# Second attention products of several token tiles in one row: a two-block fp32 kernel on one core

## The chip, the cores and the metric

The kernel runs on one core of one Trainium2 chip. The core has a matrix engine (TensorE, PE in the profile; its weight loads stand apart as PEld), three engines for elementwise work (VectorE or DVE, ScalarE or ACT, GpSimd or POOL) and a queue that only issues transfers (SyncE, SP). Each engine takes its instructions in the order of the program, and they wait for each other by semaphores. The metric is the device time of one execution in microseconds (us).

## The reference

Two transformer blocks on 1024 tokens of width 1024, in float32. What matters here is the attention, which comes in three kinds, and one small product:

```
# block 1: 8 heads of 64, banded to 256 keys per 128 queries, with sinks
m = maximum(max(scores), sink); e = exp(scores - m)
out = einsum(e / (sum(e) + exp(sink - m)), v_band)
# block 2, kind a: 8 heads, up to 640 keys per 128 queries, relative bias
probs = softmax(q @ k.T / 8 + bias);   out = probs @ v
# block 2, kind b ("stick breaking"): 8 heads, all earlier keys
weights = where(strict, exp(log_sigmoid(l) + log_tail), 0);  out = weights @ v
# modulation of block 2: one row of 6144 numbers
mod = silu(c) @ w_ada + b_ada
...
ff = square(relu(h @ w_ff1)) @ w_ff2     # the modulation is computed during this
```

## The kernel before

Nothing in the source is issued at once. A recording layer (`Recorder`) takes every instruction down; `flush` then orders them with a list scheduler that holds an estimated cost for each engine, gives a free engine the ready instruction that was recorded first, and issues the result as a fixed program. All instructions therefore carry one line number in the profile (L390, the line that calls them), and tiles are told apart by name.

Large matrix products are split: each float32 operand is a high and a low part, and three products of the parts are added (operands `128x512`, called large products below). The second product of the attention isn't split: the probabilities of a tile of 128 queries are transposed on PE in blocks of 128x128 (`PS<-cst,F`, `cst,Q`, `cst,e`, with the identity as `cst`), copied from PSUM (`PS`) to a buffer `pT` by ACT or DVE, and multiplied with V (`PS<-pT,v`). Such a product with V writes 64 rows of `PS`: one head of a pair fills rows 0 to 63, the other 64 to 127. The profile records each of them twice, so `x16` in a row of its timeline is 8 products.

The work on a pair of heads is a unit: four in block 1 (`attn1`), then four of kind b (`attn_b`), then four of kind a (`attn_a`). In a unit the tiles t = 0 to 7 follow each other: scores, softmax or stick breaking, and `pv_pair`, which takes two key blocks at a time: four transposes, one copy, four products, and then the next two blocks. There are two `pT` buffers, and every third copy is DVE's. Four tiles share one bank of PSUM for their outputs, which `o_evac` (or the end of `attn1`) empties.

PE has other work meanwhile: the large products for q and k of the next unit (`PS<-ga,low`, `PS<-low`) and, in the last unit, the first half of the output product (`PS<-low,ga`), whose operand is loaded from `d_o` into the buffers `ga` as soon as the last q and k products have read them.

The stage of `w_ff1` (products in a Winograd scheme, some 84 large products for each pair of column blocks p) computes the modulation on the side. `ada_unit` loads 256 KB of `w_ada` into one of two halves of a buffer `fxt`, and DVE multiplies it into an accumulator; after eight of them two products with a column of ones (`PS<-fxt,ones`) sum the accumulator, once for each of 12 groups.

In `attn_a` a bias tile is made for each head from a small transfer (`pT<-d_ext`), and the exponentials lie in six buffers that `attn_b` uses too.

Of the kernel before, what the change touches and what calls it, by code (L numbers as in the profile page):

```python
# [9 lines left out]
F32 = mybir.dt.float32  # L10
# [77 lines left out]
class Recorder:  # L88
# [23 lines left out]

    SIZES = {"pT": 512, "aff": 256, "ss": 2}
# [134 lines left out]
    def link(self, idx):  # L248
# [156 lines left out]
def two_blocks_kernel(ctx: ExitStack, tc: tile.TileContext, a, out, dbg=None):  # L405
# [432 lines left out]
    def pv_pair(pool, o, ocol, v, vsl, pt, kbs, t0):  # L838


        first, last = kbs[0], kbs[-1]
        for i in range(0, len(kbs), 2):
# [4 lines left out]
            sb = rec.tile(pool, [P, 512], F32, "pT", 2, uniq("pT"))  # L847
# [5 lines left out]
            j = 0  # L853
            for kb in grp:
                for hf in (0, 1):
                    PE.matmul(o[64 * hf:64 * hf + 64, ocol], v[:, kb, vsl(hf)], sb[:, j * P:j * P + P],
                              start=(kb == first), stop=(kb == last))
                    j += 1

    def attn1(i, qs):  # L860
        c = i // 2
        for t in range(NT):
# [28 lines left out]
            if t % 4 == 0:  # L891
                o = ps_o()
            ocol = slice((t % 4) * P, (t % 4) * P + P)
            kbs = list(range(t - nb + 1, t + 1))
            pv_pair(p1, o, ocol, v1, lambda hf: slice(64 * c, 64 * c + 64),
                    lambda hf, kb: e[:, hf, (kb - kbs[0]) * P:(kb - kbs[0] + 1) * P], kbs, t)
            if t % 4 == 3:
                oh = rec.tile(p1, [P, 2, 512], F32R, "oh", 2, uniq("oh"))
                ACT.copy(oh[:, 0, :], o)
                DVE.tensor_tensor(oh[:, 1, :], o, f32(oh[:, 0, :]), ALU.subtract)  # L900
                c0 = (t // 4) * 512
                SP.dma_start(f32(d_o1[i][:, :, c0:c0 + 512]), f32(oh))
# [6 lines left out]


    for t in range(NT):
# [5 lines left out]
        st = p1f()  # L917
        for n, sl in enumerate(halves):
            g = ps_g()
            gemm_N_half(g, [(pt[:, 0, k], pt[:, 1, k]) for k in range(2)], [ws.slot(I_PLE + k) for k in range(2)], n)  # L920
            ACT.copy(st[:, sl], g)
        SP.dma_start(d_ple[t], st)
# [307 lines left out]
    ada_units = [(g_, k) for g_ in range(12) for k in range(8)]  # L1230

    def ada_unit(g_, k):
        acc, w = hs(fx[0])[g_ % 2], hs(fx[1])[k % 2]
# [5 lines left out]
        if k == 7:  # L1239
            o = View.of(R_8, uniq("ada"))  # L1240
            brow = rec.tile(ff, [P, 256], F32, "aff", 1, uniq("brow"))
            for j in range(2):
                pr = slice(32 * j, 32 * j + 1)
                PE.matmul(o[pr, 0:256], ones1, acc[:, 256 * j:256 * j + 256], start=True, stop=True)
            for j in range(2):
                pr, at = slice(32 * j, 32 * j + 1), 512 * (g_ % 2) + 256 * j
                SP.dma_start(brow[pr, :], a["b_ada_2"][0:1, (g_ // 2) * 1024 + at:(g_ // 2) * 1024 + at + 256])
                DVE.tensor_tensor(brow[pr, :], o[pr, 0:256], brow[pr, :], ALU.add)
                SP.dma_start(d_ada[g_ // 2:g_ // 2 + 1, at:at + 256], brow[pr, :])
# [14 lines left out]
    def ff1_evac(p, c1, c2):  # L1264
# [6 lines left out]
        for _ in range(8 if p > 2 else 0):  # L1271
            if ada_units:
                ada_unit(*ada_units.pop(0))
# [198 lines left out]
    R_F = Ring([p7.tile([P, 1024], F32, name=f"F{i}") for i in range(4)] + [res[i] for i in (4, 5)])  # L1472
    res67 = resx[3].rearrange("p a b -> p (a b)")
    R_bA = Ring([res67[:, 640 * i:640 * i + 640] for i in range(3)])
# [48 lines left out]
    def attn_b(i, qs, ks, kl, v):  # L1523
        for t in range(NT):
# [18 lines left out]
            if t % 4 == 0:  # L1543
                o = ps_o()
            pv_pair(p7, o, slice((t % 4) * P, (t % 4) * P + P), v, lambda hf: slice(64 * hf, 64 * hf + 64),
                    lambda hf, kb: wts[hf][:, kb * P:kb * P + P], list(range(t + 1)), t)
            if t % 4 == 3:
                o_evac(4 + i, t, o, cst[:, C_GB + i:C_GB + i + 1])

    def attn_a(i, qs, ks, kl, v):  # L1550
        bias = []
        for hf in (0, 1):
            h = 2 * i + hf
            hk = rec.tile(p7, [P, 256], F32, "pT", 2, uniq("hk"))
            src = d_ext[h]
            SP.dma_start(hk, bass.AP(tensor=src.tensor, offset=src.offset + 1, ap=[[1, P], [1, 256]]))
            b = View.of(R_bA, uniq("bA"))
            DVE.tensor_copy(b[:, 0:384], hk[:, 255:256].to_broadcast([P, 384]))
            DVE.tensor_copy(b[:, 384:640], hk[:, ::-1])
            DVE.memset(b[0:64, 576:640], NEG)  # L1560
            DVE.memset(b[64:128, 0:64], NEG)
            bias.append(b)
        for t in range(NT):
            nb = min(t, 4)
            k0, nk, b0 = (t - nb) * P, (nb + 1) * P, (4 - nb) * P
            es = [p7f(), p7f()]
# [18 lines left out]
            if t % 4 == 0:  # L1585
                o = ps_o()
# [214 lines left out]
```

## Time and profile before

| | |
|---|---|
| median of 3 runs | 2362.85 us (2362.24 to 2362.9) |
| the profiled execution's own time | 2360.25 us |
| its span in the profile | 2358.5 us |
| PE busy / PE weight loads / DVE / ACT / POOL | 96% / 77% / 76% / 47% / 28% |
| block 1 attention, about | 111 to 192 us |
| stage with the modulation, about | 420 to 657 us |
| kind b attention, about | 1198 to 1413 us |
| kind a attention, about | 1413 to 1600 us |

The span is what the trace covers; the time of the execution is 1.75 us longer, and the median of the runs 2.6 us above that execution. Rows of the timeline merge equal instructions that follow each other; the start of a row less the start of the row before it is what the earlier row took of PE, since the lengths that are shown overlap.

### The profile page before, as it was taken

What the parts mean: (1) busy time and instruction counts of PE and PEld (TensorE: products, weight loads), DVE (VectorE), ACT (ScalarE), POOL (GpSimd) and SP (SyncE); (2) the same over time, 40 slices, a digit from 0 to 9 for tenths busy, and PEclk for the clock granted to TensorE, in tenths of its full rate; (3) what the DMA queues carried; (4) which work ended last, traced back from release to release, by engine and by line L of the source; (5) the groups of instructions that cost most, each with busy time, mean ns of one, the idle gap of its engine ahead of it and who ended that gap; (6) DMA issues with size and microseconds to landing.
All of it is one profiled execution on the core that took longest, in us unless ns stands there. A gap on an engine that the chain in (4) does not pass through costs nothing.

```text
span 2358.5 us, 30684 instructions
## 1 busy us (share of the span) xinstructions
PE 2259.0 (96%) x11201; PEld 1819.6 (77%) x11201; DVE 1783.6 (76%) x2613; ACT 1105.7 (47%) x1966; POOL 654.5 (28%) x541
## 2 busy tenths in 40 slices
PE   7999999999999999999999999989899999999996
PEld 6777878777778888887877777767788888887885
DVE  6464497777677889946779986663888878779897
ACT  3264275445455340055546665530855555546412
POOL 5443200000034233624535443352100000003365
PEclk9999999999999999999999999999999999999998
DMA  5529146666562316232062233363322222234123
GB/s 199 150 87 350 54 139 223 229 200 211 193 234 72 143 31 207 73 119 81 12 210 76 73 93 97 86 208 103 119 92 93 83 81 87 83 126 173 41 98 134
DMA packets 109463, 304.53 MB, mean 129 GB/s; under 512 B 11296, under 2 KB 22784, under 8 KB 106368
## 3 DMA queue, kind: packets, MB, share of 16 engines
q1 hardware_dynamic: 109312, 302.57, 38.8%
q8 instruction: 88, 1.44, 0.3%
q14 instruction: 63, 0.52, 0.1%
HBM read 211.26 MB, written 74.49 MB: 121 GB/s over the span
## 4 chain that ended last, share of the span: by engine, by line
PE 74%; DVE 10%; DMA 8%; ACT 3%; issue 2%; POOL 2%; SPq 0%; POOLq 0%; DVEq 0%; ACTq 0%
PE PS L390 74%; DMA fxt<-in_w_ada_dram 4%; DVE Q L390 3%; DVE low L390 2%; ACT Q L390 1%; DVE fxt L390 1%; POOL low L390 1%; DMA gu<-lt 1%; DMA wr<-in_w_in_dram 1%; DMA gu<-d_r 1%; DVE F L390 0%; DMA sc<-in_xT_dram 0%; DMA ga<-d_o 0%; DMA pT<-d_ext 0%; ACT low L390 0%
## 5 line engine op out<-in xcount | busy, mean ns | idle before, releaser
L390 PE MATMUL PS<-low 128*128 128x512 f32 x2868 | 686.0, 392 | 5.3 <-ACT low L390 3.7
L390 PEld LDWEIGHTS PS<-low 128*128 128x128 f32 x2868 | 537.1, 189 | 117.5 <-ACT low L390 5.2
L390 PE MATMUL PS<-ga,low 128*128 128x512 f32 x1488 | 394.0, 403 | 18.4 <-ACT ga L390 6.6
L390 PEld LDWEIGHTS PS<-ga,low 128*128 128x128 f32 x1488 | 279.6, 193 | 78.3 <-issue 14.4
L390 POOL TENSOR_TENSOR ra<-ga 128x1024 f32<-128x1024 f32 x9 | 25.2, 2801 | 786.0 <-DMA ga<-in_w_down_dram 413.1
L390 PE MATMUL PS<-gu,low 128*128 128x512 f32 x744 | 178.2, 392 | 4.5 <-POOL gu L390 4.5
L390 PEld LDWEIGHTS PS<-gu,low 128*128 128x128 f32 x744 | 140.0, 189 | 36.1 <-POOL gu L390 5.0
L390 ACT CAST low<-Q 128x512 fp32r<-128x512 f32 (+1 forms) x148 | 94.3, 640 | 151.0 <-PE PS L390 106.1
L390 PE MATMUL PS<-low,gu 128*128 128x512 f32 (+2 forms) x640 | 149.0, 384 | 2.3 <-DMA gu<-lt 1.0
L390 DVE SCALAR_TENSOR_TENSOR fy<-Q,cst,fy 128x1023 f32<-128x1023 f32 (+1 forms) x88 | 116.8, 1329 | 39.6 <-ACT fy L390 38.8
L390 PEld LDWEIGHTS PS<-low,gu 128*128 128x128 f32 x640 | 115.9, 188 | 26.5 <-issue 1.6
L390 DVE TENSOR_TENSOR low<-Q,low 128x512 fp32r<-128x512 f32 (+1 forms) x148 | 105.0, 712 | 29.8 <-ACT low L390 28.9
L390 ACT COPY Q<-PS 128x512 f32<-128x512 f32 x200 | 115.8, 579 | 24.2 <-PE PS L390 24.2
L390 PE MATMUL PS<-ra,low 128*128 128x512 f32 x480 | 120.2, 397 | 3.2 <-ACT ra L390 2.1
L390 DVE TENSOR_TENSOR Q<-PS,Q 128x512 f32<-128x512 f32 x162 | 108.7, 683 | 15.8 <-PE PS L390 14.4
L390 DVE TENSOR_TENSOR low<-ra,low 128x1024 fp32r<-128x1024 f32 x76 | 106.4, 1422 | 17.4 <-ACT low L390 17.3
L390 PE MATMUL PS<-rb,low 128*128 128x512 f32 x468 | 112.9, 390 | 2.2 <-DVE Q L390 2.2
L390 ACT CAST low<-ra 128x1024 fp32r<-128x1024 f32 x72 | 73.6, 1051 | 80.3 <-PE PS L390 67.6
L390 PEld LDWEIGHTS PS<-ra,low 128*128 128x128 f32 x480 | 91.4, 191 | 24.5 <-ACT ra L390 2.9
L390 DVE TENSOR_TENSOR low<-wr,low 128x512 fp32r<-128x512 f32 (+1 forms) x99 | 84.9, 860 | 28.5 <-POOL low L390 15.6
L390 PEld LDWEIGHTS PS<-rb,low 128*128 128x128 f32 x468 | 87.7, 188 | 21.2 <-DVE Q L390 2.6
L390 PE MATMUL PS<-low,ga 128*128 128x512 f32 x384 | 94.4, 398 | 9.1 <-DMA ga<-d_o 6.3
(270 smaller groups left out, 4291.5 us busy)
## 6 DMA issues: line engine op xcount, KB each, us to landing
fxt<-in_w_ada_dram SPq DMA_DIRECT2D x96, 256.0 KB
d_r<-Q SPq DMA_DIRECT2D x32, 512.0 KB
Q<-in_w_up_dram SPq DMA_DIRECT2D x28, 512.0 KB
d_o<-oh SPq DMA_DIRECT2D x24, 512.0 KB
d_x<-Q SPq DMA_DIRECT2D x24, 512.0 KB
wr<-in_w_in_dram SPq DMA_DIRECT2D x22, 512.0 KB
d_r<-fy SPq DMA_DIRECT2D x22, 512.0 KB
Q<-in_w_ff_dram SPq DMA_DIRECT2D x20, 512.0 KB
```

Of the source, the lines that this page charges most:

```text
L390: op["ins"] = op["fn"](*op["args"], **op["kw"])
```

## The change

`pv_pair` is split in two. `pt_tiles` transposes and copies as before, into a larger ring of buffers; `Values` holds back the products with V until the tiles up to a given t (`ends`) are copied, and then records them in one go, each of them made to wait for all of the copies (`rec.gate`). In block 1 the ends are t = 3 and 7, in block 2 t = 3, 5 and 7, and in the last unit every t. The buffers are 4 in block 1 and 8 in block 2 (they lie in `res[0]` to `res[3]`). All copies of kind b are ACT's; of the others every second one is DVE's. Of 184 copies DVE has 52 after and 61 before, in kind a 36 of 72 after and 24 before. Kind b has 8 buffers where it had 6, kind a 8 smaller ones of its own. Its bias is loaded straight into the bias tile, of which there are four instead of three; they lie in buffers that kind b uses. The modulation has four load buffers instead of two, its two summing products are recorded one p later (`ada_out`), and the outputs of the small product `d_ple` are stored in halves.

```diff
-        self.ops.append(dict(eng=eng, fn=fn, args=args, kw=kw, pri=idx + self.offset, name=name))
+        self.ops.append(dict(eng=eng, fn=fn, args=args, kw=kw, pri=idx + self.offset, name=name, gate=self.gate))
...
+        deps.update(op["gate"])
...
-    def pv_pair(pool, o, ocol, v, vsl, pt, kbs, t0):
+    def pt_tiles(ring, kbs, pt, all_act):
...
-            if evt[0] % 3:
+            if all_act or evt[0] % 2:
                 ACT.copy(sb[:, :n * P], ps[:, :n * P])
             else:
                 DVE.tensor_copy(sb[:, :n * P], ps[:, :n * P])
...
+        def add(self, t, kbs, pt):
+            self.todo.append((t, kbs, pt_tiles(self.ring, kbs, pt, self.all_act)))
+            if t not in self.ends:
+                return
+            rec.gate = [i for _, _, (_, evacs) in self.todo for i in evacs]
+            for t, kbs, (sbs, _) in self.todo:
+                if t % 4 == 0:
+                    self.o = ps_o()
+                ocol = slice((t % 4) * P, (t % 4) * P + P)
+                for kb, hf, x in sbs:
+                    PE.matmul(self.o[64 * hf:64 * hf + 64, ocol], self.v[:, kb, self.vsl(hf)], x,
+                              start=(kb == kbs[0]), stop=(kb == kbs[-1]))
+            rec.gate = []
...
+        values = Values(R_pT1, (3,7), v1, lambda hf: slice(64 * c, 64 * c + 64), evac)
...
-        acc, w = hs(fx[0])[g_ % 2], hs(fx[1])[k % 2]
+        acc, w = hs(fx[0])[g_ % 2], (hs(fx[1]) + hs(fx[2]))[k % 4]
...
+        if 0 <= p - 4 < 12:
+            ada_out(p - 4)
+        if 0 <= p - 3 < 12:
+            for k in range(8):
+                ada_unit(p - 3, k)
...
-    R_F = Ring([p7.tile([P, 1024], F32, name=f"F{i}") for i in range(4)] + [res[i] for i in (4, 5)])
+    R_F = Ring([fs[:, 1024 * i:1024 * i + 1024] for i in range(4)] + [res[i] for i in (4, 5, 6, 7)])
+    R_E = Ring([fs[:, 640 * i:640 * i + 640] for i in range(6)] + [rs[2][:, 640 * i:640 * i + 640] for i in (0, 1)])
+    R_bA = Ring([rs[3][:, 640 * i:640 * i + 640] for i in range(3)] + [rs[2][:, 1280:1920]])
...
+    R_pT2 = Ring([x for t in range(4) for x in hs(res[t])])
+    R_pT3 = Ring(hs(res[3]) + rec.ring[id(p7), "pT"].tiles)
...
-            SP.dma_start(hk, bass.AP(tensor=src.tensor, offset=src.offset + 1, ap=[[1, P], [1, 256]]))
+            SP.dma_start(b[:, 0:256], bass.AP(tensor=src.tensor, offset=src.offset + 1, ap=[[1, P], [1, 256]]))
...
+        plan = (R_pT2, (3,5,7)) if n_ < 7 else (R_pT3, range(NT))
```

Three places show what this does to the order on PE. The first is in the first unit of kind a, on PE, before: large products, transposes (`cst`) and products with V (`64x128`).

```order
L390 MATMUL PS<-cst,F_8031 128x128
L390 MATMUL PS<-kl_0_8021,gu_5_2115 128x128
L390 MATMUL PS<-low 128x512 x5
L390 MATMUL PS<-pT_0_8023,v_1_8027 64x128 x4
L390 MATMUL PS<-cst,Q_2_122 128x128
L390 MATMUL PS<-pT_1_8024,v_1_8027 64x128 x2
L390 MATMUL PS<-cst,Q_2_122 128x128
L390 MATMUL PS<-low 128x512 x2
L390 MATMUL PS<-cst,F_8030 128x128
```

The products with V come two, four or six at a time, between other work. The same engine after the change, at the end of the second unit of kind a (the buffers of transposed probabilities are now called `Q`):

```order
L393 MATMUL PS<-cst,Q_2_122 128x128 x4
L393 MATMUL PS<-ga_5_2122,low 128x512 x2
L393 MATMUL PS<-cst,Q_2_122 128x128 x2
L393 MATMUL PS<-ga_5_2122,low 128x512
L393 MATMUL PS<-low 128x512 x4
L393 MATMUL PS<-Q_2_121,v_1_8035 64x128 x8
L393 MATMUL PS<-Q_2_120,v_1_8035 64x128 x12
L393 MATMUL PS<-low 128x512 x8
```

Twenty products now follow each other, five large products behind the last transpose. In the whole program they stand in 135 unbroken rows before (2 to 8 products each; 95 of them are followed by a transpose) and in 37 after (most of 14 to 30), 8, 12 and 17 of them in block 1, kind b and kind a, where there were 29, 56 and 50; runs of transposes are 265 before and 269 after.

The second place is the stage of the modulation, on PE, from one pair of summing products to the next; before:

```order
L390 MATMUL PS<-fxt,ones_69 1x256 x2
L390 MATMUL PS<-rb_2072,low 128x512 x4
L390 MATMUL PS<-ga_1_87,low 128x512 x12
L390 MATMUL PS<-rb_2072,low 128x512 x8
L390 MATMUL PS<-low 128x512 x12
L390 MATMUL PS<-ga_1_88,wx 128x512 x12
L390 MATMUL PS<-gu_1_86,wx 128x512 x12
L390 MATMUL PS<-gu_1_85,low 128x512 x9
L390 MATMUL PS<-fxt,ones_69 1x256 x2
```

Between the two pairs are 69 large products (63 to 93 elsewhere). After:

```order
L393 MATMUL PS<-fxt,ones_69 1x256 x2
L393 MATMUL PS<-low 128x512 x12
L393 MATMUL PS<-ga_1_88,wx 128x512 x12
L393 MATMUL PS<-gu_1_86,wx 128x512 x12
L393 MATMUL PS<-gu_1_85,low 128x512 x12
L393 MATMUL PS<-ga_1_87,low 128x512 x12
L393 MATMUL PS<-ra_2079,low 128x512 x12
L393 MATMUL PS<-rb_2080,low 128x512 x12
L393 MATMUL PS<-fxt,ones_69 1x256 x2
```

Here they are 84, and so at nine of the eleven intervals; the first interval has 31 (71 before) and the last 48. Counted in large products, the first pair stands 18 earlier than before, the second 58 earlier and the last 20 later.

The third place is PE at the start of the last unit, where the output product (`low,ga`) begins; before:

```order
L390 MATMUL PS<-low 128x512 x12
L390 MATMUL PS<-ga_5_2113,low 128x512 x6
L390 MATMUL PS<-ga_5_2114,low 128x512 x6
L390 MATMUL PS<-low 128x512 x12
L390 MATMUL PS<-low,ga_5_2113 128x512 x2
```

and after, from the last reader of `ga_5_2121`, with a row of products with V between:

```order
L393 MATMUL PS<-ga_5_2121,low 128x512 x5
L393 MATMUL PS<-Q_2_120,v_0_8034 64x128 x14
L393 MATMUL PS<-Q_2_121,v_0_8034 64x128 x6
L393 MATMUL PS<-ga_5_2122,low 128x512 x6
L393 MATMUL PS<-low 128x512 x12
L393 MATMUL PS<-gu_5_2124,gu_5_2123 128x128
```

Behind that last line come 19 more score products (128 to 512 columns each, `gu` and `kl`) and three transposes, and only then `low,ga`.

## Rows read from the trace of the kernel before

**Rows 1.** The page, part 1: busy time, share of the span, instructions.

```profile
PE 2259.0 (96%) x11201; PEld 1819.6 (77%) x11201; DVE 1783.6 (76%) x2613; ACT 1105.7 (47%) x1966; POOL 654.5 (28%) x541
```

**Rows 2.** Who PE waited for, whole span: us in total, times, longest.

```profile
PE PS L390 <- DVE fxt L390: 15.6, 10, 3.4
```

**Rows 3.** By stretch: us, then busy of PE, PEld, DVE, ACT, POOL; granted clock; DMA.

```profile
1198.00:1413.00 215.00, 214.26 (x1475) 165.81 (x1475) 193.85 (x211) 134.96 (x293) 102.41 (x141) 0.99 0.34 94
1413.00:1600.00 187.00, 173.66 (x1206) 131.43 (x1203) 125.89 (x449) 91.55 (x214) 76.82 (x85) 0.98 0.46 138
```

**Rows 4.** Groups of PE instructions: busy us, mean ns, idle before.

```profile
L390 PE MATMUL PS<-pT,v 128*64 128x128 f32 x1296 | 100.8, 283 | 1.7 <-DVE oh L390 0.9 <-DVE pT L390 0.6 <-ACT pT L390 0.2
```

**Rows 5.** The chain that ended last: start us, us, what.

```profile
1709.90 405.14 PE PS L390 x1786
```

**Rows 6.** Timeline of PE in kind a: start us, us.

```profile
1457.02 1.09 PE L390 MATMUL PS<-pT,v 128*64 128x128 f32 x16
1458.05 0.33 PE L390 MATMUL PS<-cst,Q 128*128 128x128 f32 x1
1458.21 0.27 PE L390 MATMUL PS<-cst,F 128*128 128x128 f32 x1
1458.24 1.40 PE L390 MATMUL PS<-low 128*128 128x512 f32 x5
1459.57 0.44 PE L390 MATMUL PS<-pT,v 128*64 128x128 f32 x4
1459.94 1.89 PE L390 MATMUL PS<-low 128*128 128x512 f32 x7
1461.66 0.39 PE L390 MATMUL PS<-ga,low 128*128 128x512 f32 x1
```

**Rows 7.** Timeline of PE in kind b: a large product ahead of products with V.

```profile
1298.76 0.39 PE L390 MATMUL PS<-ga,low 128*128 128x512 f32 x1
1299.08 1.09 PE L390 MATMUL PS<-pT,v 128*64 128x128 f32 x16
```

**Rows 8.** Timeline of PE in kind a: last transposes, and products that waited for the copy.

```profile
1452.48 0.27 PE L390 MATMUL PS<-cst,Q 128*128 128x128 f32 x1
...
1453.61 0.44 PE L390 MATMUL PS<-pT,v 128*64 128x128 f32 x4 [0.17 <-ACT pT L390]
```

**Rows 9.** DVE's copies to `pT`, from 1198 to 1413 us.

```profile
L390 DVE COPY pT<-PS 128x512 f32<-128x512 f32 x20 | 13.7, 683 | 3.4 <-PE PS L390 3.2
...
L390 DVE COPY pT<-PS 128x256 f32<-128x256 f32 x7 | 2.9, 415 | 2.5 <-PE PS L390 2.3
```

**Rows 10.** Who waited, from 1413 to 1600 us: DVE, then PE.

```profile
DVE Q L390 <- DMA pT<-d_ext: 13.4, 5, 4.0
...
PE PS L390 <- DVE m L390: 2.8, 6, 1.2
```

**Rows 11.** Tile `fxt`: who waited for its loads (us, times).

```profile
  DVE fxt L390: 52.4, 47
```

**Rows 12.** Timeline of PE: the summing products, first, second and last of 12 groups.

```profile
447.05 0.60 PE L390 MATMUL PS<-fxt,ones 128*1 128x256 f32 x4
...
464.86 0.60 PE L390 MATMUL PS<-fxt,ones 128*1 128x256 f32 x4 [0.47 <-DVE fxt L390]
...
656.45 0.60 PE L390 MATMUL PS<-fxt,ones 128*1 128x256 f32 x4 [1.54 <-DVE fxt L390]
```

**Rows 13.** Stretches at a lower granted clock, columns as in rows 3.

```profile
540.60:544.00 3.40, 3.40 (x9) 2.65 (x9) 2.56 (x5) 1.10 (x2) 0.00 (x0) 0.50 0.76 247
...
1557.80:1564.60 6.80, 5.08 (x15) 3.98 (x16) 4.90 (x14) 0.88 (x4) 0.00 (x0) 0.50 1.00 261
```

**Rows 14.** Timeline of PE and SP where the output product begins.

```profile
1547.64 2.88 PE L390 MATMUL PS<-ga,low 128*128 128x512 f32 x12
...
1548.51 0.64 SPq L390 DMA_DIRECT2D ga<-d_o  x1
...
1559.50 0.77 PE L390 MATMUL PS<-low,ga 128*128 128x512 f32 x1 [6.26 <-DMA ga<-d_o]
```

More of the change, by code (lines that the diff above doesn't have):

```diff
@@ L836, in two_blocks_kernel @@
     evt = [0]
-    def pv_pair(pool, o, ocol, v, vsl, pt, kbs, t0):
-        first, last = kbs[0], kbs[-1]
+    def pt_tiles(ring, kbs, pt, all_act):
+        sbs, evacs = [], []
         for i in range(0, len(kbs), 2):
@@ L852, in pv_pair, with __init__, evac @@
                 DVE.tensor_copy(sb[:, :n * P], ps[:, :n * P])
[L853 to L858, printed above, removed]
+            evacs.append(len(rec.ops) - 1)
+            sbs += [(kb, hf, sb[:, (2 * j + hf) * P:(2 * j + hf + 1) * P]) for j, kb in enumerate(grp) for hf in (0, 1)]
+        return sbs, evacs
+    class Values:
+        def __init__(self, ring, ends, v, vsl, evac, all_act=False):
+            self.ring, self.v, self.vsl, self.ends, self.evac, self.todo = ring, v, vsl, ends, evac, []
+            self.all_act = all_act
+        def add(self, t, kbs, pt):
[11 more added lines that the diff above has]
+            rec.gate = []
+            if t % 4 == 3:
+                self.evac(t, self.o)
+            self.todo = []
+    R_pT1 = Ring([sc1[:, 512 * i:512 * i + 512] for i in range(4, 6)] +
+                 [p1.tile([P, 512], F32, name=f"pT{i}") for i in range(2)])
     def attn1(i, qs):
         c = i // 2
+        def evac(t, o):
+            oh = rec.tile(p1, [P, 2, 512], F32R, "oh", 2, uniq("oh"))
+            ACT.copy(oh[:, 0, :], o)
+            DVE.tensor_tensor(oh[:, 1, :], o, f32(oh[:, 0, :]), ALU.subtract)
+            c0 = (t // 4) * 512
+            SP.dma_start(f32(d_o1[i][:, :, c0:c0 + 512]), f32(oh))
+        values = Values(R_pT1, (3,7), v1, lambda hf: slice(64 * c, 64 * c + 64), evac)
         for t in range(NT):
@@ L890, in attn1 @@
                 POOL.tensor_scalar(e[:, hf, :nk], e[:, hf, :nk], den[:, hf:hf + 1], 1.0, ALU.mult, ALU.mult)
-            if t % 4 == 0:
-                o = ps_o()
-            ocol = slice((t % 4) * P, (t % 4) * P + P)
             kbs = list(range(t - nb + 1, t + 1))
[L895 to L902, printed above, removed]
+            values.add(t, kbs, lambda hf, kb: e[:, hf, (kb - kbs[0]) * P:(kb - kbs[0] + 1) * P])
     for i in range(4):
@@ L908, in two_blocks_kernel @@
         attn1(i, qs)
+    R_st = Ring([sc1[:, 512 * i:512 * i + 512] for i in range(4)])
     for t in range(NT):
@@ L1238, in ada_unit, with ada_out @@
             DVE.scalar_tensor_tensor(acc, w, cact[:, k:k + 1], acc, ALU.mult, ALU.add)
[L1239 to L1249, printed above, removed]
+    def ada_out(g_):
+        acc = hs(fx[0])[g_ % 2]
+        o = View.of(R_8, uniq("ada"))
+        brow = rec.tile(ff, [P, 256], F32, "aff", 1, uniq("brow"))
+        for j in range(2):
+            pr = slice(32 * j, 32 * j + 1)
+            PE.matmul(o[pr, 0:256], ones1, acc[:, 256 * j:256 * j + 256], start=True, stop=True)
+        for j in range(2):
+            pr, at = slice(32 * j, 32 * j + 1), 512 * (g_ % 2) + 256 * j
+            SP.dma_start(brow[pr, :], a["b_ada_2"][0:1, (g_ // 2) * 1024 + at:(g_ // 2) * 1024 + at + 256])
+            DVE.tensor_tensor(brow[pr, :], o[pr, 0:256], brow[pr, :], ALU.add)
+            SP.dma_start(d_ada[g_ // 2:g_ // 2 + 1, at:at + 256], brow[pr, :])
     def h1_tiles(p):
```

51 lines of the change are left out of this document (20 added, 31 removed).

## The prediction

> **What bounds the kernel now.** I read the page's busy times first: PE 96%, the next engine 76% [rows 1]. A busy share doesn't say that an engine sets the pace, so the waits of PE come next; the span less PE's busy time leaves 99 us of idle PE, and the largest single cause is the summing products of the modulation, 15.6 us in ten waits [rows 2]. In the attention stages PE hardly waits: 0.7 us in 215 of kind b, 13 in 187 of kind a [rows 3], and 1.7 us at all products with V together [rows 4]. So there a microsecond counts if it leaves PE's own row of work, and the timeline has to say what a product with V costs beyond its columns.
>
> **What a row of such products costs.** Undisturbed, a large product takes 405.14 / 1786 = 0.227 us [rows 5]. Eight products with V take 1458.05 - 1457.02 = 1.03 us and two take 1459.94 - 1459.57 = 0.37 [rows 6], so 0.11 each and 0.15 once for the row. The large product ahead of a row takes 0.32 instead of 0.227, 0.09 more [rows 7]. Behind a row, seven large ones take 1461.66 - 1459.94 = 1.72 instead of 1.59, 0.13 more; where a transpose follows, it takes 0.16 instead of the 0.11 that transposes take in a run, 0.05 more, with the next one's 0.03 ahead of a large product as without a row [rows 6]. A row thus costs 0.15 + 0.09 + 0.05 = 0.29 us ahead of a transpose and 0.37 ahead of other work, whatever its length.
>
> **The change, part by part.**
> *Rows.* Of the 135 rows 95 end at a transpose and 40 elsewhere: 95 x 0.29 + 40 x 0.37 = 42.4 us, 0.314 each. After the change there are 37, 98 fewer: **-30.8 us** (6.6 in block 1, 13.8 in kind b, 10.4 in kind a). Products and transposes stay as many, and runs of transposes grow by 4 of 265, which I leave out.
>
> *The gate.* Each row now waits for all copies of its tiles. Behind it on PE stand the large products, the next transposes and scores, so a late copy stops everything. From the last transpose to products that had waited 0.17 us for ACT's copy there passed 1453.61 - 1452.48 = 1.13 us [rows 8]: that is what a copy needs. The order after puts five large products there at the place shown, 1.13 us and 0.1 to 0.2 for what transposes and rows add around them, as the order before does. With that margin the 135 rows waited 1.7 us in all [rows 4]; 37 have fewer occasions, but each waits for a whole group, and copies of the next tiles wait until the row has freed buffers. Lower bound 0, upper 0.35 us a row, as much as a row's own price: 13 us. I take **+3**, nearer the row of 1.7.
>
> *Copies.* Kind b's 27 copies on DVE (13.7 + 2.9 = 16.6 us [rows 9]) go to ACT, which rises from 135 to about 152 us (at DVE's lengths) of some 201; DVE falls from 194 to 177 [rows 3]. In kind a DVE gets 36 of 72 copies instead of 24: 12 x 0.68 = 8 us on 126 of 187. Both stay below PE, which hides them; without that cover they would cost these 15 and 8 us.
>
> *Buffers for softmax and bias.* DVE waits 13.4 us for bias transfers in kind a, and PE 2.8 us for DVE's softmax [rows 10]. With four bias tiles the loads can start earlier; I take half of PE's share, **-1.4** (bounds 0 and 2.8). The first kind a unit is the exception: its bias now lies in buffers of kind b and waits for the last transposes of kind b. Late then are its first scores, while PE has the next unit's 96 large products (22 us) ahead; the longest such wait of DVE was 4.0 us [rows 10], and I put **+1.5** on PE (bounds 0 and 4). The bias loads wait in SP's queue, and behind them stand weights of the next units, which have that same cover.
>
> *Modulation.* With two buffers DVE waits 52.4 us for loads [rows 11], and PE for DVE. From first to last group it takes 656.45 - 447.05 = 209.4 us [rows 12], 19.0 a group. After the change 84 large products lie between two sums, 84 x 0.227 + 0.6 = 19.7 us, so from the third group on the old pace of loads would be enough, and four buffers can only be faster. The second group is different: its sum stands 58 large products, 13 us, earlier than before, where it waited 0.47 [rows 12]. At the old pace it waits 13.6 us; at double pace (four buffers for two) a group needs 9.5 us, 7.0 of which the interval of 31 gives, so 2.5. I take 3.6 and gain **-12** (bounds -2 and -15.6). Behind two of the old waits the granted clock fell to 0.50 for 3.4 us (one of the two in [rows 13]), the level of 1.2 GHz, which costs half of it, 1.7 us each: I count one, **-1.7** (bounds 0 and -3.4).
>
> *Start of the output product.* The first `ga` buffer is last read three products into 1547.64, at 1548.3; its load is issued at 1548.51 and PE goes on at 1559.50, after 6.26 us of waiting [rows 14]: 11.2 us from release to use. After the change PE has, from that release, 3 + 6 + 12 large products (4.8 us), a row of 20 products with V (20 x 0.11 + 0.37 = 2.6) and the scores with their transposes (5888 columns at 0.227 per 512, and 3 x 0.11: 2.9), together 10.3 us. So 0.9 is left of the wait: -5.4. Of the 6.8 us at the lower clock behind it PE was busy 5.08 [rows 13], half of which, 2.5, goes too if the clock holds; I take 1.6 of it, **-7** together (bounds 0 and -8.8).
>
> *At no cost.* The split `d_ple` stores are eight more issues on SP, in a stage where the order after has large products to run; one such issue takes SP 0.64 us [rows 14], so 5 us if all of it were bare.
>
> **The sum.** -30.8 + 3 - 1.4 + 1.5 - 12 - 1.7 - 7 = -48.4 us. From 2360.25, the profiled execution's own time (span 2358.5 and 1.75 around it), that is 2311.9; the median of the runs was 2.6 above that execution, so 2314.
>
> **Rivals.**
> *DVE sets the pace of the second attention.* PE's 96% overstates it if weight loads (77%) are the measure. In kind b DVE is at 194 of 215 us. For: its scans and PE are both nearly full. Against: in kind a DVE idles 61 us, and PE waits for its softmax 2.8. If DVE kept its shares of 90% and 67%, kind b would last 177 / 0.90 = 197 us, 18 less, and kind a 134 / 0.67 = 200, 13 more: -5 where the rows give -24.2. Time: 2333. The Trainium skill, in Perfetto Trace Analysis, Identifying the Most-Contended Engine, says the same of such shares: matmul busy time is a poor measure and the weight loads' share a better one, by which PE has room here and DVE in kind b doesn't. The trace agrees on the shares, but PE's 0.7 us of idleness in kind b speaks for rows that cost PE time of their own.
> *Products of the two heads run side by side in long rows.* They fill different halves of `PS`. For: nothing but those halves differ. Against: eight in a row, four of each half, take 1.03 us, 0.11 each as in any length [rows 6]. If pairs ran together, 648 products would take 648 x 0.055 = 36 us less: 2278. In the Trainium skill, TensorEngine Tiling (Array Packing), Key Properties, different tiles of the array can run in parallel; no row here shows it.
> *The modulation only moves its wait.* The second sum waits 13.6 us, with a clock stretch, and the output product's load still comes late: -12 and -7 shrink to -2 and 0, -1.7 to 0, and new waits are 5 instead of 4.5: -30.8 - 2 - 1.4 + 5 = -29.2, time 2333.
> *Slower: the gate starves PE.* Place: between last transpose and row. For: each row needs up to eight copies, on an ACT queue that also has kind b's sigmoids, and two PSUM banks feed them. The price is what each of 37 rows waits; it decides from (48.4 + 3) / 37 = 1.4 us a row on. At 2 us a row it is 74 in place of 3: 2314 + 71 = 2385. Against: five large products of cover in the order, and 1.7 us for 135 rows before.
> That the rows don't come about is excluded by the order.
>
> **How the numbers follow.** The likeliest case has 0.72 and its own range 2301 to 2328: all gains at their bounds and no new wait give -61.4; new waits of 10, the modulation at -8 and the output product at -3.5 give about -34. DVE's pace 0.08, the moved wait 0.11, side by side 0.02, slower 0.05, nothing of note 0.02. From 2300 to 2337 lie most of the likeliest case and of the two cases at 2333, whose prices have errors of their own: some 8 in 10. A measurement can tell 0.2%, about 5 us, from no change: faster 0.93, same 0.02, slower 0.05.
>
> **What would show it.** In the trace of after: 37 rows of products with V, a product still at 0.11 us, rows still costing 0.3; waits of PE at them under 5 us; the wait on `fxt` at 2 to 6 us and only at the second group; the first `low,ga` product waiting under 2 us; kind b near 201 us long, with DVE at some 177 busy. Wrong I am if PE waits for copies between transposes and rows, if kind a grows longer than 177 us, or if rows get their price back inside, by products of more than 0.11.

## The result, and the profile after

The median of four runs is 2329.14 us (2328.22 to 2334.03), beside 2362.55 for the kernel before: a ratio of 0.9868, with a 95% interval from 0.9848 to 0.9888. A second set of five runs, taken apart from these, gave 2332.91 beside 2358.35, 0.9892 (0.9875 to 0.9909). The gain is thus 25 to 33 us where I forecast 48. The sign held, and both medians lie within the 2300 to 2337 that I gave some 8 in 10; they lie just above the 2301 to 2328 that I gave the likeliest case, so the sum was some 15 to 23 us too good.

The page of the profiled execution (2334.03 us, span 2332.3), part 1, in the form of [rows 1]:

```profile
PE 2233.1 (96%) x11201; PEld 1828.5 (78%) x11201; DVE 1775.5 (76%) x2604; ACT 1109.0 (48%) x1975; POOL 663.8 (28%) x541
```

PE's busy time fell from 2259.0 to 2233.1, by 25.9. The span less PE's busy time was 99.5 us and is 99.2 (95.1 and 93.5 in a second trace of each kernel, described below), and the mean granted clock is 0.985 in both. So the gain is PE's own work, and of the 18 us of idle time and lower clock that the forecast wanted to save next to nothing is left in the sum. A table by stage says where it went. The edges are the same events in both kernels: last product with V of block 1 (it stands at 212 us before, so the attention of block 1 reaches beyond the 192 us given for it above); 420 and 660 us; the wait at the end of the feed-forward part (`ga,low`); the last products with V of kind b and of kind a. Columns as in [rows 3]. Before:

```profile
0.00:212.50 212.50, 191.57 (x1052) 147.45 (x1052) 127.02 (x386) 94.21 (x261) 94.62 (x114) 0.97 0.55 177
212.50:420.00 207.50, 201.99 (x903) 165.58 (x900) 133.49 (x222) 103.70 (x189) 23.92 (x18) 0.98 0.48 169
420.00:660.00 240.00, 222.65 (x970) 174.87 (x969) 170.32 (x268) 111.39 (x160) 2.39 (x1) 0.99 0.65 212
660.00:1198.40 538.40, 524.54 (x2358) 432.73 (x2358) 425.37 (x392) 213.94 (x299) 213.70 (x106) 0.99 0.32 112
1198.40:1413.00 214.60, 214.12 (x1475) 165.64 (x1475) 193.48 (x210) 134.96 (x293) 102.41 (x141) 0.99 0.34 94
1413.00:1604.00 191.00, 177.66 (x1237) 134.18 (x1233) 127.34 (x451) 92.38 (x215) 76.82 (x85) 0.98 0.46 135
1604.00:2358.50 754.50, 726.47 (x3223) 599.18 (x3220) 606.54 (x688) 355.11 (x549) 140.68 (x76) 0.99 0.29 99
```

After:

```profile
0.00:207.40 207.40, 182.87 (x1051) 145.64 (x1051) 125.99 (x392) 90.39 (x254) 94.00 (x114) 0.99 0.56 178
207.40:420.00 212.60, 203.31 (x904) 165.50 (x901) 133.91 (x222) 104.26 (x190) 23.89 (x18) 0.98 0.48 168
420.00:660.00 240.00, 233.01 (x1026) 184.25 (x1025) 187.38 (x277) 122.99 (x171) 9.97 (x4) 0.99 0.71 242
660.00:1182.00 522.00, 510.56 (x2299) 421.99 (x2299) 413.26 (x382) 203.68 (x288) 207.75 (x104) 0.99 0.30 101
1182.00:1389.00 207.00, 203.98 (x1491) 171.78 (x1491) 183.52 (x197) 144.72 (x323) 109.96 (x141) 0.98 0.33 89
1389.00:1575.00 186.00, 170.00 (x1222) 138.55 (x1219) 123.86 (x451) 87.33 (x201) 76.94 (x85) 0.96 0.46 145
1575.00:2332.30 757.30, 729.38 (x3220) 600.76 (x3218) 607.55 (x688) 355.58 (x549) 141.24 (x76) 0.98 0.29 100
```

Block 1 with all ahead of it is 5.1 us shorter; the middle (rows two to four) 985.9 - 974.6 = 11.3; the second attention, kinds b and a, 405.6 - 393.0 = 12.6; the rest 2.8 longer. PE's idle time (length less busy) fell by 10.4 where the modulation is computed, and by 2.4 in the stage behind that, and rose by 3.8 in the stage behind block 1, by 2.5 in kind b and by 2.7 in kind a. (It rose by 3.6 in block 1 too, but not in the second traces.) The second attention holds most of the miss: the forecast has -28.1 there (-13.8 and -10.4 for rows, +3, -1.4, +1.5, -7).

The products with V themselves, the group of [rows 4], now under three names of their buffers:

```profile
L393 PE MATMUL PS<-Q,v 128*64 128x128 f32 x1004 | 61.1, 276 | 0.0
L393 PE MATMUL PS<-pT,v 128*64 128x128 f32 x180 | 12.6, 280 | 0.0
L393 PE MATMUL PS<-sc,v 128*64 128x128 f32 x112 | 7.9, 280 | 0.0
```

They are busy for 81.6 us instead of 100.8, and nothing waits ahead of them: the gate costs 0.0 there. A whole row of 30 products, from the timeline of PE at the end of kind b:

```profile
1385.68 3.50 PE L393 MATMUL PS<-Q,v 128*64 128x128 f32 x60
1389.10 0.38 PE L393 MATMUL PS<-ones,sqacc 128*128 128x1 f32 x2
```

3.42 us; 30 x 0.11 + 0.15 would be 3.45. The price of a product is as forecast, and no pair of heads runs side by side.

The modulation: DVE's waits for the loads ([rows 11] before), here for the half of the four buffers that is still called `fxt`, and the first pair of sums in the timeline:

```profile
  DVE fxt L393: 7.0, 10
...
444.19 0.75 PE L393 MATMUL PS<-fxt,ones 128*1 128x256 f32 x4 [3.06 <-DVE fxt L393]
```

The other half lies in a buffer `fx`, for whose loads DVE waits 2.1 us, so 9.1 in all where it was 52.4. PE's wait for the sums fell from 15.6 in ten to 3.06 in one, and that is at the first group, not at the second. One stretch of 3.4 us at a clock of 0.50 follows it, at 444.5 us, where there were two in this stage before.

What the second attention lost. First, small waits at the head of its units. The chain of waits through the last unit (start us, us, what):

```profile
1518.91 4.93 DMA kl<-kl
1525.53 11.29 DMA kl<-kl
...
1551.83 1.77 DVE m L393
1553.77 2.02 DVE low L393
```

The output product's operand is no longer what PE waits for. But the scores that I had counted as cover need halves of k that a transfer of 128 KB moves within the chip, and one of these took 11.29 us from issue to use, while the loads of `ga` (4 MB) passed. Then come VectorE's maximum (`m`) and the operand made of w_out (`low`).

Second, behind these waits the granted clock falls. Five stretches in kinds b and a after, columns as before:

```profile
1229.60:1233.00 3.40, 3.07 (x14) 2.67 (x14) 3.34 (x4) 1.49 (x3) 2.31 (x2) 0.50 0.02 5
1393.40:1396.80 3.40, 3.40 (x13) 3.01 (x12) 2.18 (x12) 1.20 (x4) 0.66 (x2) 0.50 0.40 152
1526.50:1529.90 3.40, 3.29 (x9) 2.30 (x10) 2.74 (x17) 1.09 (x4) 1.66 (x2) 0.51 0.99 374
1536.80:1540.20 3.40, 3.34 (x11) 2.88 (x12) 1.11 (x4) 1.22 (x4) 1.34 (x2) 0.50 0.98 399
1557.30:1560.70 3.40, 3.40 (x24) 3.07 (x21) 1.97 (x4) 0.26 (x1) 3.21 (x3) 0.50 0.65 188
```

With 3.2 us at the start of kind b they are 20.2 us at 0.50, the level of 1.2 GHz; before there were 4.4 us at the start of kind b and the 6.8 us of [rows 13], 11.2. Half of such a stretch is lost: 10.1 instead of 5.6. (In the second traces of each, below, the stretches are 25.8 and 14.7 us, so the difference holds.) So -24.2 for rows, +5.2 of idle time and +4.5 of clock make -14.5 in this stage, beside -12.6 measured.

### The profile page after: what moved, and what is told of

It reads as the page before. It is cut to its first block, busy times and chain, and to the rows that moved or that the text cites. A ratio compares the mean times of both kernels' runs of the same rounds, so it can differ in the third digit from the quotient of the medians.

```text
span 2332.3 us, 30737 instructions
## 1 busy us (share of the span) xinstructions
PE 2233.1 (96%) x11201; PEld 1828.5 (78%) x11201; DVE 1775.5 (76%) x2604; ACT 1109.0 (48%) x1975; POOL 663.8 (28%) x541
## 4 chain that ended last, share of the span: by engine, by line
PE 77%; DVE 11%; DMA 5%; ACT 2%; POOL 2%; issue 2%; SPq 0%; POOLq 0%; DVEq 0%; ACTq 0%
PE PS L393 77%; DVE Q L393 4%; DVE low L393 2%; ACT Q L393 1%; POOL low L393 1%; DMA kl<-kl 1%; DVE bn L393 1%; DMA gu<-lt 1%; DMA wr<-in_w_in_dram 1%; DMA gu<-d_r 1%; POOL Q L393 1%; DMA sc<-in_xT_dram 1%; ACT gu L393 0%; DVE ga L393 0%; DVE wr L393 0%
## 5 line engine op out<-in xcount | busy, mean ns | idle before, releaser
L393 PE MATMUL PS<-ga,low 128*128 128x512 f32 x1488 | 389.7, 401 | 17.8 <-ACT ga L393 7.3
L393 ACT COPY Q<-PS 128x512 f32<-128x512 f32 (+1 forms) x312 | 174.2, 567 | 70.1 <-PE PS L393 69.5
L393 DVE TENSOR_TENSOR Q<-PS,Q 128x512 f32<-128x512 f32 x162 | 108.9, 685 | 13.7 <-PE PS L393 12.6
L393 DVE TENSOR_TENSOR low<-wr,low 128x512 fp32r<-128x512 f32 (+1 forms) x99 | 85.8, 869 | 30.4 <-ACT low L393 15.8
L393 POOL TENSOR_SCALAR low<-wr 128x1024 fp32r<-128x1024 f32 (+1 forms) x45 | 55.6, 1236 | 169.9 <-PE PS L393 123.0
```

Of the source, the lines that this page charges most:

```text
L393: op["ins"] = op["fn"](*op["args"], **op["kw"])
```

## The experiments

All edits start from the kernel after, where nothing else is said. The order is made anew by the list scheduler for each of them, so an edit can also move work that it doesn't name. The times of one kernel lie 0.2 to 0.6% apart, so totals are compared by their ratios to the kernel before on the same chip, and stages by the traces.

**Once more, both kernels.**

> The changed kernel as it is, once more, as the mark for the kernels beside it. Its profiled execution (2334.0) lay 4 to 6 us above its other three times (2328.2 to 2329.8). If that surplus is chance, it comes out near 2329 here; if the profiled one is the rule, near 2334. In the trace the stall in the last unit (PE's waits from 1523 to 1556 us: 1.33, 1.76, 3.25 and smaller ones) and the waits at the stores of the small product (1.44 and 1.51 at 215 and 218 us) should come back within 1 us if they belong to the program, and not if they are chance.

2332.91, as given above. The waits came back at the same products: 1.33, 2.25 and 3.25 us in the last unit (1.33, 1.76 and 3.25 in the first trace), 2.09 behind the small product's stores, there in one instead of two. They belong to the program. The surplus of the first profiled execution is chance: here the profiled one is the median of 2330.46 to 2336.93.

> The kernel before, profiled once more, as the mark for stages that no edit touches: from the last sum of the modulation to kind b, and from the last product with V to the end, after and three of its variants spent 4 us more in the last of these than the one trace of before. If that is chance of the one trace, this trace shows 743 to 746 us there (741.3 in the first); if the change makes it slower, 741 again.

```profile
1604.10:2362.50 758.40, 731.91 (x3224) 603.57 (x3220) 605.26 (x688) 355.06 (x549) 140.06 (x76) 0.98 0.29 99
```

The last stage took 758.4 us here and 754.5 in the first trace, so the rest's loss of 2.8 us lies within what two executions of before differ by (this one took 2364.28, 4.2 above the median of its eight). The second attention took 406.6, as in the first trace (405.6).

**The modulation alone**, on the kernel before:

```diff
-        acc, w = hs(fx[0])[g_ % 2], hs(fx[1])[k % 2]
+        acc, w = hs(fx[0])[g_ % 2], (hs(fx[1]) + hs(fx[2]))[k % 4]
...
+        if 0 <= p - 4 < 12:
+            ada_out(p - 4)
```

> The kernel before with the modulation's part of the change alone (four load buffers, sums recorded one p later). The trace of after says that the wait before the sums was 15.6 us in ten and is 3.1 in one, and no lower clock is left in that stage: by that 16 us less than before, a ratio of 0.993. My forecast was 13.7 us less (0.994). The rival that the wait only moves expects 2 us less, 0.999.

2346.81 us, 0.9946 (0.9931 to 0.9961): 12.7 us less than before (9.2 to 16.3). The same stage:

```profile
420.00:660.00 240.00, 233.03 (x1033) 184.51 (x1032) 188.39 (x275) 123.93 (x173) 13.27 (x5) 1.00 0.71 241
```

PE idles 7.0 us there as in after. No lower clock is left in this trace's stage; in that of after one stretch is, against what the expectation says. This term of the forecast (-13.7) was right, and the rival that the wait only moves was wrong here.

**What a row is worth.** Shorter rows, and rows without the gate:

```diff
-        values = Values(R_pT1, (3,7), v1, lambda hf: slice(64 * c, 64 * c + 64), evac)
+        values = Values(R_pT1, range(NT), v1, lambda hf: slice(64 * c, 64 * c + 64), evac)
...
-        plan = (R_pT2, (3,5,7)) if n_ < 7 else (R_pT3, range(NT))
+        plan = (R_pT2, range(NT)) if n_ < 7 else (R_pT3, range(NT))
```

> After, with the products with V recorded at every tile t in all units: 93 unbroken rows instead of 37, 62 of them followed by a transpose, nothing else changed. If a row costs PE 0.29 to 0.37 us of its own whatever else goes on, the order costs 17.7 us more, and the time is 15 to 19 us above after. If VectorE or the scalar engine set the pace of the attention, the rows' price comes back only in part: 0 to 6 us above after. If the gate starves PE, the time is not above after, since every wait is then for fewer copies.

```diff
-            rec.gate = [i for _, _, (_, evacs) in self.todo for i in evacs]
```

> After without the gate: the products of several tiles are still recorded behind their transposes, but each waits for its own copy alone. The order then has 152 unbroken rows of products with V instead of 37, 57 of them followed by a transpose. If the rows themselves carry the price (0.29 ahead of a transpose, 0.37 elsewhere), the order costs 36 us more, and the time is 30 to 38 us above after, even above before. If long rows gain only because of more buffers and later products, the time stays within 6 us of after. If the gate makes PE wait, it falls below after.

Part 1 of the page of each, first with rows at every tile, then without the gate:

```profile
PE 2251.0 (96%) x11201; PEld 1827.1 (78%) x11201; DVE 1780.6 (76%) x2604; ACT 1108.1 (47%) x1975; POOL 666.6 (28%) x541
PE 2269.4 (96%) x11201; PEld 1832.2 (78%) x11201; DVE 1773.8 (75%) x2604; ACT 1107.8 (47%) x1975; POOL 663.8 (28%) x541
```

With 93 rows 2344.04 us, 0.9932 (0.9914 to 0.9951); with 152 rows 2358.59, 0.9997 (0.9988 to 1.0005), as slow as before although buffers, copies and modulation are those of after. The products with V in the latter:

```profile
L393 PE MATMUL PS<-Q,v 128*64 128x128 f32 x1004 | 80.6, 282 | 0.0
L393 PE MATMUL PS<-pT,v 128*64 128x128 f32 x180 | 18.1, 287 | 0.3 <-DVE pT L393 0.3
L393 PE MATMUL PS<-sc,v 128*64 128x128 f32 x112 | 9.9, 287 | 0.0
```

108.6 us of busy time for the same 648 products. Rows carry most of the gain, and the gate is what makes them: neither the buffers nor the later products alone do. But by the ratios to the kernel before and the second set of after, 56 rows more cost 9.4 us, 0.17 each, and 115 more 24.8 us, 0.22 each (15.1 and 30.4 us, 0.27 and 0.26 each, by the first set of after). The order counts 0.31. By the second set both times came out between the cases of their expectations, by the first at the lower edge of the case in which rows carry the price.

The traces tell what a row costs PE from what comes back as waits. Less half of the time at the lower clock (72.3 and 87.4 us in the two traces of before, 73.9 and 82.5 in those of after, 84.8 with 93 rows, 77.7 with 152), which makes it an estimate, PE is busy for 2222.9 and 2223.7 us before, 2196.2 and 2196.5 after, 2208.6 with 93 rows and 2230.6 with 152. So the 98 rows that the change saves gave some 27 us, 0.28 each, and in the two runs here a row cost 0.22 and 0.30. With the 12.7 us of the modulation that makes some 40 us, of which 25 to 33 are left. In the second attention PE idles for 13.8 us before and 19.0 after (13.2 and 19.2 between the same events in the second traces), 14.9 with 93 rows and 7.9 with 152. Some 11 us of waits thus come with the long rows and their gate, though none of them stands ahead of a row.

**The loads at the start of the output product**, cut to an eighth of their columns, and cut in halves:

```diff
-        SP.dma_start(f32(ga[k]), f32(d_o2[4 + k]))
+        SP.dma_start(f32(ga[k][:, :, 0:128]), f32(d_o2[4 + k][:, :, 0:128]))
```

> After, with the four loads of 1 MB of the attention's output at the start of the output product cut to an eighth of their columns (the rest of the operand keeps older numbers, so the output isn't the reference's). If these 4 MB, which take the transfers' whole rate for some 10 us, are what makes PE wait in the last unit (for moved halves of k, for the operand made of w_out), 8 to 12 us less than after, and the stretch of lower clock there is gone. If the scores' own chain (VectorE's maximum, the exponentials) or GpSimd sets the pace there, 0 to 3 us less.

```diff
-    for k in range(4):
-        SP.dma_start(f32(ga[k]), f32(d_o2[4 + k]))
+    for c0 in (0, 512):
+        for k in range(4):
+            SP.dma_start(f32(ga[k][:, :, c0:c0 + 512]), f32(d_o2[4 + k][:, :, c0:c0 + 512]))
```

> After with the four loads of 1 MB at the start of the output product cut in halves, first the columns of tiles 0 to 3 of all four. With the loads cut to an eighth the last unit was 3.4 us shorter than in after beside it, and the waits for moved halves of q and k (3.7 us) were gone. If what counts is only how much stands ahead of those moves in the transfers, halves give 1 to 3 us of this; if the total of 5 MB has to pass before PE can go on, nothing.

Cut to an eighth: 2333.64 us, 0.9889 (0.9871 to 0.9907), which the total doesn't tell from after. In the trace the last unit (from the last product with V of the unit before to its own last) takes 53.9 us instead of the 57.2 of after beside it (56.1 in the first trace; before 59.5 and 59.9), and PE's waits there are

```profile
PE PS L393 <- DVE m L393: 4.2, 4, 1.8
PE PS L393 <- DVE low L393: 2.4, 3, 1.6
```

The 3.7 us for moved halves, which this second trace of after has, are gone, but 6.6 of others stay. The lower clock isn't gone either: 6.8 us where it was 10.2. So the transfers are a part of the stall, not all of it, and less than the 8 to 12 us that I expected. Halves: 2331.59, 0.9882 (0.9864 to 0.9900); 53.0 us for the unit in its trace, but waits for `low` of 4.2 in place of those for the moves. One wait takes the place of the other. The profiled executions lie 5.2 and 1.9 us below the next of their four, so a part of the shorter unit may be chance.

**GpSimd beside VectorE.** The rows of w_out are multiplied by a modulation row; this moves from GpSimd to VectorE, and the rounding to the scalar engine, by a new kind of weight, `NA`:

```diff
+            if kind == "NA":
+                DVE.tensor_tensor(raw[:, cs], raw[:, cs], spec[2]()[:, cs], ALU.mult)
+                ACT.copy(slot[:, 0, cs], raw[:, cs])
...
-    specs = [("NS", a["w_out_2"][0, (4 * (1 - hb) + k) * P:(4 * (1 - hb) + k + 1) * P, :], lambda: gm)
+    specs = [("NA", a["w_out_2"][0, (4 * (1 - hb) + k) * P:(4 * (1 - hb) + k + 1) * P, :], lambda: gm)
```

> After with the rows of w_out multiplied on VectorE and rounded on the scalar engine, where GpSimd did both (2.38 and 1.05 us each). In the last unit of after a VectorE operation on 128x1 takes 1.76 us beside such a multiplication instead of 0.2, the difference of parts behind it 2.09 instead of 1.22, and PE waits 3.3 us for that. If VectorE is held up by GpSimd there, these operations take their 0.2 and 1.2 us, PE's waits for VectorE in the last unit (5.3 us) fall under 2, and the unit is 3 to 6 us shorter. If the transfers of 5 MB alone set the pace, it is as long as in after (56 to 57 us), within 2.

In its trace the difference of parts takes 1.21 to 1.22 us in the place concerned, PE's waits are

```profile
PE PS L393 <- DVE m L393: 3.2, 3, 1.9
...
PE PS L393 <- DVE low L393: 0.8, 1, 0.8
```

and the unit takes 48.4 us instead of 57.2 (56.1), although VectorE has more to do. The total is less clear: 2328.92, 0.9862 (0.9841 to 0.9883), 3 parts in a thousand below the second set of after and 0.6 below the first, with intervals that overlap; and the profiled execution, at 2321.74, lies 6.8 us below the next of the four. So the shorter unit is shown for one execution, and a faster program isn't. The wait for `low` fell as expected (3.3 to 0.8); that for `m` did not, so VectorE's waits together are 4.0 us and not under 2.

**The stores of the small product**, whole again from three full buffers:

```diff
+        st = p1f()
...
-            g, st = ps_g(), View.of(R_st, uniq("st"))
+            g = ps_g()
...
-            ACT.copy(st, g)
-            SP.dma_start(d_ple[t][:, sl], st)
+            ACT.copy(st[:, sl], g)
+        SP.dma_start(d_ple[t], st)
```

> After with the small product's outputs stored whole from three full buffers, as before, instead of in halves from four half buffers. The trace of after shows the scalar engine waiting 7.0 us for those stores between 185 and 232 us, and PE 2.3 to 3.5 us behind it. If the halved buffers are the cause, PE's waits there go and the stage from the last product with V of block 1 to the first sum is 2 to 4 us shorter; I had put this edit at nothing, which expects no difference.

2336.07 us, 0.9899 (0.9885 to 0.9914): no gain. In its trace PE waits 6.0 us for these outputs, more than in after. So the halved buffers alone aren't the cause; the nothing that I had first put on this edit fits better. (The profiled execution took 2343.12 us, 7 above the median.)

**The buffers that bias and kind b share.** Six buffers for kind b and three bias tiles of their own; then six buffers alone:

```diff
-    R_F = Ring([fs[:, 1024 * i:1024 * i + 1024] for i in range(4)] + [res[i] for i in (4, 5, 6, 7)])
+    R_F = Ring([fs[:, 1024 * i:1024 * i + 1024] for i in range(4)] + [res[i] for i in (4, 5)])
...
-    R_bA = Ring([rs[3][:, 640 * i:640 * i + 640] for i in range(3)] + [rs[2][:, 1280:1920]])
+    R_bA = Ring([rs[3][:, 640 * i:640 * i + 640] for i in range(3)])
```

> After with kind b's buffers cut from eight to six, as before, and three bias tiles that share nothing with kind b. If the late bias of the first unit of kind a (PE waits 0.9 and 2.0 us there, and the unit has some 5.5 us more of waits than before) comes from its sharing buffers with kind b, that unit is 3 to 5 us shorter and kind b at most 1 us longer. If the wait comes from the scores and exponentials that now stand ahead of products held back, nothing changes.

> After with kind b's buffers cut from eight to six, the bias tiles staying four (three of them now outside kind b's buffers). The variant that also gave up the fourth bias tile took 2322.8, 10 us less than after beside it in time, of which its trace puts 4.4 in the first unit of kind a, 1 in kind b and 5 in the last unit. If the buffers that the bias shared with kind b were the cause, this one is within 3 us of that, 2320 to 2326. If the fourth bias tile did it, 2330 to 2334, as after.

Both parts: 2322.77 us, 0.9846 (0.9833 to 0.9860), 10 us under the second set of after and clear of it; against the first set, 6 us above it, the intervals overlap. Kinds b and a in its trace, with the same number of products on PE as in after:

```profile
1179.00:1395.40 216.40, 212.85 (x1529) 178.31 (x1529) 193.23 (x225) 149.53 (x337) 108.26 (x148) 0.99 0.33 91
1395.40:1564.80 169.40, 158.32 (x1184) 128.26 (x1179) 118.62 (x422) 81.07 (x186) 72.30 (x79) 0.98 0.47 151
```

Together 385.8 us instead of 393.0 (395.2 in the second trace): idle 14.6 instead of 19.0, and the stretches of lower clock at the first units of b and of a are gone (12.9 us of them in all, where there were 20.2). The work is spread otherwise between the two kinds, so they aren't compared one by one, and the 4.4 us that I expected of the first unit of kind a can't be read there. Six buffers alone: 2328.48, 0.9857 (0.9836 to 0.9878); 389.7 us in the trace, with the last unit as long as in after. That lies between the two cases of the expectation, so what the fourth bias tile does stays open. Counted by last products with V, the units of the two traces agree within 0.4 us from the second of kind b on, but for the last: 51.5 us with three bias tiles, 56.2 with four.

**Both that helped.**

> After with both edits that shortened a stage in their traces: six buffers for kind b with three bias tiles of their own, and w_out multiplied on VectorE and rounded on the scalar engine. If the stages add up, the first unit of kind a takes 36 us (46.5 in after) with the last unit near 48 (57.2), and the time is 2314 to 2321. If what one edit saves is only the room that the other would need, it is no faster than the first of them alone, 2321 to 2326.

2321.76 us, 0.9835 (0.9819 to 0.9852); 383.8 us for kinds b and a. It is the fastest of all by a little, but not to be told from the first of the two variants before. In its trace the first unit of kind a takes 36.2 us and the last unit 49.7, near to what I expected if the stages add up; but six buffers with three bias tiles had brought the last unit to 51.5 already, so little was left there for the second edit to save.

## Why the forecast was right in sign and too large

One of my signs of being wrong came: kind a is 186.0 us long by the edges of the table (191.0 before), where I had drawn the line at 177. Of the other two neither did: PE waits for no copy ahead of a row, and a product takes 0.11 us. The terms one by one:

- **Rows, -30.8.** The mechanism and the count (37) are right, and so is a product's 0.11 us. By PE's busy time they gave some 27; net of the waits that come with them a row is worth 0.17 to 0.27 us.
- **Gate, +3.** It measured 0.0 ahead of the products. But it was too small: without the gate PE idles 11 us less in the second attention, near the upper bound of 13. I had looked for this price between transposes and rows, and it shows at scores, transposes and the products behind them. Whether the wait for all copies makes it, or the order that goes with long rows, isn't told apart. The rival in which the gate starves PE ahead of the rows is out.
- **Copies, 0.** Right: in kind b VectorE is busy 183.5 of 207 us (6.5 more than forecast), and nothing waits for a copy ahead of a row.
- **Buffers, -1.4 and +1.5.** The bias does load earlier: DVE waits for it 2.6 us in kinds b and a where it waited 13.4. But PE's wait for `m` there rose from 2.8 to 4.3 instead of falling by 1.4. In the first unit of kind a the bias is late, as forecast, and PE behind it:

```profile
1391.03 0.82 DVE L393 COPY Q<-Q 128x256 f32<-128x256 f32 x2 [1.57 <-DMA Q<-d_ext]
...
1392.48 0.39 PE L393 MATMUL PS<-gu,gu 128*128 128x256 f32 x1 [1.92 <-DVE m L393]
```

PE's waits in that unit are 4.2 us (0.8 before). I had put the next unit's 96 large products there as cover, but in the order scores stand ahead of them, and PE takes its order as it comes. The first unit of kind b, which the forecast passes over, has its own: transposes stand in the order before VectorE has made their weights.

```profile
1229.84 0.47 PE L393 MATMUL PS<-cst,Q 128*128 128x128 f32 x1 [2.92 <-DVE Q L393]
```

Each is followed by 3.4 us at a clock of 0.50 in this trace, so each costs 1.7 more than the wait itself. With six buffers for kind b both stretches go, and so does DVE's wait for the bias. That edit undoes the sharing and takes two buffers away, so for the first unit of kind b, where no bias plays a part, the cause isn't shown.
- **Modulation, -13.7.** Right in size (-12.7 alone). The wait that is left stands at the first group, whose sum now comes 18 large products earlier, and not at the second: four buffers keep ahead of it (DVE waits 9.1 us for loads where it waited 52.4).
- **Output product, -7.** This is the step whose reasoning failed: "After the change PE has, from that release, 3 + 6 + 12 large products", a row "and the scores with their transposes", "together 10.3 us. So 0.9 is left of the wait". The wait for `ga` did go: the first `low,ga` product waits 0.68. But the scores are not cover that is simply there. They wait for moved halves of q and k in the same transfers, then for VectorE's maxima, and the products behind them for w_out. In the last unit PE waits

```profile
PE PS L393 <- DVE low L393: 5.0, 2, 3.2
PE PS L393 <- DVE m L393: 1.9, 3, 1.3
PE PS L393 <- DMA kl<-kl: 1.2, 2, 1.0
PE PS L393 <- POOL low L393: 0.7, 1, 0.7
```

8.8 us, where it waited 10.0 before (9.7 and 8.8 in the second traces), with 10.2 us at the lower clock where it had 6.8 (10.2 in the second trace of before). So about 0 of the 7 came. Less load (the cut to an eighth), halves, and less of GpSimd each take away one of these waits, and the next stands behind it. How the 8.8 us would fall to nothing is open.
- **The small product, 0.** In the stage behind block 1 PE's idle time rose by 3.8 us, and the rows that show it are

```profile
215.40 1.66 PE L393 MATMUL PS<-low,plT 128*128 128x512 f32 x6 [1.44 <-ACT sc L393]
...
218.56 0.73 PE L393 MATMUL PS<-low,plT 128*128 128x512 f32 x2 [1.51 <-ACT sc L393]
```

Some 3 of the 5 us that I allowed "if all of it were bare". The scalar engine waits 7.0 us there for stores to land. Whole stores didn't help; the transfers are busy for 97% of the time from 195 to 225 us (96% before), which would hold up a stage that now starts 5 us earlier, but no run tried that.

Of the rivals, VectorE as the pace of the second attention gave 2333, near to what was measured, but not by its mechanism: it put kind b at 197 us and kind a at 200, and they are 207 and 186; with 152 rows VectorE has the work of after, and the time is 25 us longer; with w_out's products moved onto VectorE the last unit is shorter. That the modulation only moves its wait, also 2333, was wrong on the modulation; on the output product its 0 was right, but not its reason, since the load came in time. That both give a time so near to the measured one is chance.

## What to carry to other kernels

Work that PE is to do while it waits is cover only as far as its own operands are there in time; here the moved halves, the maxima and the operand made of w_out weren't. Follow the operands of the cover one step back before counting it. When a kernel's main engine gets faster, look for what its stages share at their borders (buffers, transfers in flight), since waits of 1 to 3 us at such borders, with the lower clock behind them, took back some 10 of the 24 us that the rows gave in the order. And a row of another kind of work has a price of its own on PE that no busy share shows (96% before and after): the timeline of two neighbours does.

## What I had not expected of the hardware

A VectorE operation on 128x1 lasted until a large one of GpSimd beside it ended. From the last unit of after:

```profile
1551.21 2.36 POOL L393 TENSOR_TENSOR wr<-wr,v 128x1024 f32<-128x1024 f32 x1
1551.83 1.75 DVE L393 TENSOR_TENSOR m<-m 128x1 f32<-128x1 f32 x1
1553.62 0.15 DVE L393 TENSOR_SCALAR nm<-m 128x1 f32<-128x1 f32 x1
1553.66 1.04 POOL L393 TENSOR_SCALAR low<-wr 128x1024 fp32r<-128x1024 f32 x1
1553.69 2.09 DVE L393 TENSOR_TENSOR low<-wr,low 128x1024 fp32r<-128x1024 f32 x1
...
1555.83 0.50 PE L393 MATMUL PS<-low,ga 128*128 128x512 f32 x1 [3.25 <-DVE low L393]
```

The maximum of two numbers takes 1.75 us and ends with GpSimd's multiplication (1551.21 + 2.36 = 1553.57; 1551.83 + 1.75 = 1553.58); the next operation, on the same size with one tile as input, takes 0.15. The same maximum takes 0.15 with no GpSimd operation beside it, in the run with w_out's products on VectorE; there too one that starts beside a GpSimd multiplication ends with it (1549.32 + 0.60 = 1549.12 + 0.80). The difference of parts takes 2.09 instead of the 1.22 that it took with GpSimd's two operations moved away. The Trainium skill says in SBUF — State Buffer, Who interferes with whom, that a VectorE instruction with two inputs in SBUF contends with a GpSimd instruction that reads SBUF, and it calls contention for the ports that the two share an exclusive lock. The first pair agrees to 0.01 us; the second is longer by 0.87, a little less than the 1.01 that were left of GpSimd's operation when it started.

A move of 128 KB within the chip took 11.29 us from issue to use, issued between loads of 4 MB; no row shown of before has it, since PE waited for the load itself there.
